# Memory tokens of the last four row tiles: from matrix-engine transposes to strips that the vector engine turns

## The chip, the core and the metric

The kernel runs on one core of a Trainium2 chip. A core has a matrix engine (TensorE, PE in the profile; its weight loads are listed as PEld), a vector engine (VectorE, DVE), a scalar engine (ScalarE, ACT), GpSimd (POOL) and SyncE (SP), which here only issues transfers. Sixteen DMA engines move data between the device's memory and the core's on-chip memory. The metric is device time of one execution in microseconds (us).

## The reference, cut to what matters

Two layers of an encoder over 256 positions of width 2048, each with three groups of heads (a gated convolution, a differential attention, a cross attention into 256 memory tokens). What the change touches is how the memory tokens become keys and values, which depends on `mem` and the weights alone and not on the layer's `x`:

```python
for l in range(DEPTH):                       # DEPTH = 2
    h = rmsnorm(x, norm_g[l]); proj = h @ w_in[l]
    ...
    mn = rmsnorm(mem, mem_norm_g[l])         # mem: 256 x 2048
    mkv = mn @ w_mem_kv[l]                   # 2048 x 1024: 512 columns of keys, 512 of values
    mk = rmsnorm(keys of mkv, per head of 128); mv = values of mkv
    ...                                      # attention of 4 heads into mk, mv
    x = x + y @ w_out[l]
```

All numbers are float32. The kernel multiplies them as pairs of parts, a high one (`hi`, the number rounded to the engine's short format) and a low one (`lo`, the rest), in three products: hi by hi, token lo by weight hi, token hi by weight lo.

## The kernel before

**Three stages.** The first stage makes keys and values of both layers out of the memory tokens (some 97 us, matmuls of line 743, `products`). Then come the two layers, whose matmuls are those of `block` (lines 301 to 303). Every matmul of `block` and of `products` moves 512 columns.

**The first stage** goes over 32 row tiles, named g = 0 to 31: 16 row tiles k of 128 rows of `w_mem_kv` for layer 0, then 16 for layer 1. Row tile g takes 12 matmuls: `products(g, 0, ...)` for the keys' half (two halves of the tokens, times three products) and `products(g, 1, ...)` for the values' half. The order within one g >= 3 is written out by hand: the first two matmuls of the keys' half, then `operands(g + 2)`, then the other four, then `beside(g)`, then six of the values' half, then `run_side()`. For k = 14 and 15, and for the first two row tiles of layer 1, the values' half is moved to a later place.

**`operands(n)`** makes what row tile n multiplies. `token_parts(n)`, for n < 16 alone, brings the tokens into columns: two 128x128 transposes on TensorE (line 721, into tile `pt`), an ACT copy (L252) to `memT`'s hi part and a DVE subtraction (L253) for its lo part. `memT` is kept, so layer 1 needs no token work. `w_parts(n)` scales the weights by the gain: ACT writes `hi` (L715), DVE writes `lo` (L716). ACT and DVE work through their own instructions strictly in this order. There are four buffers each for `raw`, `hi` and `lo`, so SP's load of `raw` for row tile g + 4 (L707, issued in `beside(g)`) waits until DVE has written `lo` of row tile g.

**`beside(g)`** holds what lies next to the products: loads of the tokens, four row tiles at a time (L701, in their natural layout, `xs`), loads of the weights, one small constant at a time from a list (L776), the tokens' squares on ACT (L661, at g = 4, 8, 11 and 13), natural loads of `x` at g = 18, 21, 24, 27 (L764), whose squares (L650) follow three row tiles later, and at g = 4, 9, 14, 19 the start of `x_turned` for one quarter of `x` each. `x`'s squares are not pinned to a place; the planner of the program puts them in ACT's order.

**`x_turned`** brings a quarter of `x` (512 columns) into columns without TensorE: four DMAs (L618) fetch strips (each partition takes pieces of 128 numbers, 512 bytes), two row tiles later one DVE instruction turns them in 32x32 blocks (L622), and in the next two `run_side` calls ACT (L255) and DVE (L256) write hi and lo parts of two column tiles each. Row j of such a tile is row 4p + j of its quarter and not row 128j + p, so the weights that meet it are loaded by `x_row_tiles` in the same order. Tile tags `e` (the strips) and `sh` (the turned tile) have two buffers each.

**The start**: `weights(0)` to `weights(3)` and tokens 0 to 3 are loaded in an order written out by hand; the first row tiles go in halves (`w_parts(g + 1, 0, NB)`, then `w_parts(g + 1, NB, NB)`), while `weights(2)` and `weights(3)` come in one transfer each and tokens 2 and 3 together.

Of the kernel before, what the change touches and what calls it, by code (L numbers as in the profile page):

```python
# [11 lines left out]
F32 = mybir.dt.float32  # L12
# [7 lines left out]
P = 128  # L20
D_MODEL = 2048
SEQ = 256
DEPTH = 2
NT = SEQ // P
KT = D_MODEL // P
# [8 lines left out]
NB = 512  # L34
CK = 2
PARTS = 8
B = 32
NA = P // B
PAIR_EVERY = 9
QT = NB // P  # L40


C_X, C_B, C_C, C_G = 0, 768, 1536, 2304
# [5 lines left out]
def encoder(ctx: ExitStack, tc: tile.TileContext, x, mem, norm_g, w_in, conv_w, conv_b,  # L49
            dq_g, dk_g, lq1, lk1, lq2, lk2, head_g, mem_norm_g, w_mem_kv, mq_g, mk_g, w_out, out):  # L50
    nc = tc.nc
    x, mem, out = x[0], mem[0], out[0]

    def pool(name, bufs, space=None):
        kw = {"space": space} if space is not None else {}
        return ctx.enter_context(tc.tile_pool(name=name, bufs=bufs, **kw))

    const = pool("const", 1)
# [3 lines left out]
    tmp = pool("tmp", 2)  # L62
# [8 lines left out]
    def nm(s):  # L71
        uid[0] += 1
        return f"{s}_{uid[0]}"
# [8 lines left out]
    def distance(t):  # L82
        tc.keep_in_program_order(nc.scalar.activation(dist[:, t], dist[:, t], AF.Abs))
# [13 lines left out]
    def on_all_rows(v):  # L97
        return v.rearrange("l d -> (l d)").unsqueeze(0).to_broadcast([P, DEPTH * HALF])
# [3 lines left out]
    pin = tc.keep_in_program_order  # L102

    def small_loads():

        yield gx.rearrange("p (m j) -> p m j", j=QT), norm_g.rearrange("l (q p j) -> p (l q) j", p=P, j=QT)
        for r0, v in vb_rows:
            n, w = v.shape
            for j in range(P // w):
                yield vb[r0:r0 + n, j * w:(j + 1) * w], v  # L110
        for j, v in enumerate((lq1, lk1, lq2, lk2)):
            yield lam_in[:, j, :], on_all_rows(v)

    constants = small_loads()


# [7 lines left out]
    cva = const.tile([P, 32], F32, name="cva")  # L124

    def g_norm(l, k):
        return gx[:, l * KT + k:l * KT + k + 1]

    def g_mnorm(l, k):
        return cva[:, l * KT + k:l * KT + k + 1]  # L130

    cvb = const.tile([P, 64], F32, name="cvb")
    hgain = const.tile([P, DEPTH], F32, name="hgain")
# [71 lines left out]
    def later(g, n):  # L205
        due[id(g)] = chunk[0] + n
        return g
# [40 lines left out]
    def split_T(dst, k, src, gain, pin=False):  # L248

        hi, lo = dst[:, 0, k, :], dst[:, 1, k, :]  # L250
        if gain is None:
            both = (nc.scalar.copy(hi, src),  # L252
                    nc.vector.tensor_tensor(lo, src, hi.bitcast(F32), ALU.subtract))  # L253
        else:
            both = (nc.scalar.activation(hi, src, AF.Copy, scale=gain),  # L255
                    nc.vector.scalar_tensor_tensor(lo, src, gain, hi.bitcast(F32), ALU.mult, ALU.subtract))  # L256
        if pin:
            for i in both:
                tc.keep_in_program_order(i)
        made.add((id(dst), k))  # L260
# [5 lines left out]
    def x_row_tiles(w, k):  # L266

        q, j = divmod(k, QT)
        return w[q * NB:(q + 1) * NB].rearrange("(p j) c -> p j c", j=QT)[:, j:j + CK]

# [155 lines left out]
    def strips(v):  # L426
        return v.rearrange("p (b c) -> p b c", c=B)
# [180 lines left out]
    def mem_out(h, yn, po, r, a):  # L608
        for i in range(NT):
            nc.vector.scalar_tensor_tensor(yn[:, :, i], strips(po[:, i, :]), r[:, i:i + 1],  # L610
                                           strips(a[:, i, h * P:(h + 1) * P]), ALU.mult, ALU.mult)

    def x_turned(dst, l, q, src):


        st = tmp.tile([P, SEQ // B, B * QT], F32, tag="e", name=nm("xt"))
        for b in range(NA):
            tc.keep_in_program_order(nc.sync.dma_start(  # L618
                st[b * B:(b + 1) * B], src[:, b * B * QT:(b + 1) * B * QT].rearrange("(n p) r -> p n r", p=B)))
        yield 2  # L620
        whole = tmp.tile([P, QT, SEQ], F32, tag="sh", name=nm("xf"))
        tc.keep_in_program_order(nc.vector.transpose(whole.rearrange("p j (n i) -> p j n i", i=B),  # L622
                                                     st.rearrange("p n (c j) -> p j n c", j=QT)))
        yield
        for j in range(QT):
            split_T(dst, q * QT + j, whole[:, j], g_norm(l, q * QT + j), pin=True)
            if j % 2:
                yield
# [13 lines left out]
    def T_tile(what):  # L642
        kept.append(big.tile([P, 2, KT, SEQ], F32R, tag="T", name=nm(what)))
        return kept[-1]
# [9 lines left out]
    memT = T_tile("memT")  # L654
    ssm = const.tile([P, NT, 4], F32, name="ssm")

    def mem_squares(c):

        for t in range(NT):
            sq = tmp.tile([P, NB], F32, tag="nat", name=nm("msq"), bufs=3)  # L660
            pin(nc.scalar.activation(sq, xs[:, t, c * NB:(c + 1) * NB], AF.Square, accum_out=ssm[:, t, c:c + 1]))  # L661
# [35 lines left out]
    mkT, mv, away, raws, parts = [], [], [], {}, {}  # L697
    xT = T_tile("xT")

    def tokens(k, n):  # L700
        pin(nc.sync.dma_start(xs[:, :, k * P:(k + n) * P], mem[:, k * P:(k + n) * P].rearrange("(t p) c -> p t c", p=P)))  # L701

    def weights(g, at=0, n=2 * NB, eng=nc.sync):
        l, k = divmod(g, KT)
        if g not in raws:
            raws[g] = wp.tile([P, CK, NB], F32, tag="raw", name=nm("raw"), bufs=4)
        pin(eng.dma_start(raws[g].rearrange("p h c -> p (h c)")[:, at:at + n],  # L707
                          w_mem_kv[l][k * P:(k + 1) * P, at:at + n]))

    def w_parts(g, at=0, n=2 * NB):  # L710
        if g not in parts:
# [6 lines left out]
    def turned(k):  # L718
        pt = ps_t.tile([P, SEQ], F32, tag="t", name=nm("pt"))
        for t in range(NT):  # L720
            pin(nc.tensor.transpose(pt[:, t * P:(t + 1) * P], xs[:, t, k * P:(k + 1) * P], ident))  # L721
        return pt

    def token_parts(g):
        if g < KT:
            split_T(memT, g, turned(g), None, pin=True)

    def operands(g):
        token_parts(g)
        w_parts(g)  # L730
# [36 lines left out]
    def beside(g):  # L767


        if g + 4 < NG:  # L770
            if g % QT == 0 and g + QT < KT:
                tokens(g + QT, QT)
            weights(g + 4)
        if g >= 3:
            for dst, src in islice(constants, 1):
                pin(nc.sync.dma_start(dst, src))  # L776
        if g in (4, 9, 14, 19):
            q = g // 5
            tasks.append(later(x_turned(xT, 0, q, x[:, q * NB:(q + 1) * NB]), 1))
        if g in (4, 8, 11, 13):  # L780
            mem_squares((4, 8, 11, 13).index(g))
        if g == 6:
            distance(1)
        if g == 13:
            tasks.append(later(mem_stats(), 1))
        if g == 28:
            rest_of_constants()
        if g > KT and (g - KT) % 3 == 2 and g < 30:
            x_natural((g - KT) // 3)
        if g > 20 and (g - KT) % 3 == 2:  # L790
            for t in range(NT):
                x_square((g - KT) // 3 - 1, t)

    for _ in range(DEPTH):
        l = len(mkT)
# [6 lines left out]
    tokens(1, 1)  # L802
    weights(1, 0, NB)
    weights(1, NB, NB)
    tokens(2, 2)
    weights(2)
    weights(3)
    warm(5)
    distance(0)
# [24 lines left out]
    for g in range(3, NG):  # L834
        l, k = divmod(g, KT)
# [19 lines left out]
    for l in range(DEPTH):  # L855
        st = stats_of(ssx, "st")
# [146 lines left out]
        for b in range(4):  # L1003
# [3 lines left out]
            for t in range(NT):  # L1007
                n = 256 if final else NB
                for lo in range(0, NB, n):
                    xc = xs[:, t, b * NB + lo:b * NB + lo + n]  # L1010
                    nc.vector.tensor_tensor(xc, acc[t][:, lo:lo + n], xc, ALU.add)  # L1011
                    if final:
                        eng = nc.scalar if lo else nc.sync
# [36 lines left out]
```

## Time and profile before

| | |
|---|---|
| median of 3 runs | 923.13 us (922.33 to 924.15) |
| the profiled execution's own time | 922.7 us |
| its span, first to last instruction | 920.9 us |
| busy: PE / DVE / ACT | 99% / 73% / 54% of the span |
| bytes moved | 215.06 MB, mean 234 GB/s |
| first stage | from 4.76 us to about 97.4 us |

Times in the trace are us from the span's start. PE's sum of busy time is that of pipelined instructions; the distance from one start to the next says what an instruction costs the engine. A row of the timeline is a start, a length, an engine, a line and an operation, the tile written `<-` the tiles read, and in square brackets the idle time ahead of it with what ended it. A `q` behind the engine's name marks an issue of its queue. The chain of waits gives start, length, engine, tile, line and count.

### The profile page before, as it was taken

To read this page: it belongs to the slowest core of one execution; us is meant where nothing else is said; L and a number is where in the kernel's file an instruction comes from. 1 tells how busy PE (TensorE), PEld (TensorE's weight loads), DVE (VectorE), ACT (ScalarE), POOL (GpSimd) and SP (SyncE) were. 2 spreads that over 40 slices of the span, in tenths; PEclk is the share of its full clock that TensorE was granted. 3 is DMA by queue.
4 is the path that set the end of the run, shared out by engine and by line. 5 is a ranking of instruction groups with operands and counts; after the bars stand their busy time and mean duration, and the time that the engine had idled before them with its cause. 6 is when DMAs were issued, how large, how long until landed. Compare 5 with 4: busy or idle time off the path is not lost.

```text
span 920.9 us, 12319 instructions
## 1 busy us (share of the span) xinstructions
PE 915.9 (99%) x4192; PEld 761.0 (83%) x4192; DVE 671.9 (73%) x1195; ACT 501.9 (54%) x770; POOL 7.0 (1%) x18
## 2 busy tenths in 40 slices
PE   9999999999999999999999999999999999999998
PEld 7888888888888888888888888888888888888886
DVE  5797877857898787467676757878898777468652
ACT  6676645675545554436455544568555554446431
POOL 0001000000000000000000000000000000000000
PEclk9999999999999999999999999999999999999999
DMA  8988877876679997989677767885889897989662
GB/s 280 273 257 298 267 234 231 259 208 197 175 219 243 234 278 235 242 263 257 222 262 241 240 197 218 234 236 182 238 231 223 254 237 209 250 252 262 214 223 68
DMA packets 250226, 215.06 MB, mean 234 GB/s; under 512 B 131166, under 2 KB 176820, under 8 KB 250164
## 3 DMA queue, kind: packets, MB, share of 16 engines
q1 hardware_dynamic: 248004, 210.72, 78.7%
q0 software_dynamic: 672, 2.10, 0.6%
q10 hardware_dynamic: 1488, 1.46, 0.5%
q8 instruction: 33, 0.54, 0.2%
q14 instruction: 29, 0.24, 0.1%
HBM read 193.26 MB, written 20.97 MB: 233 GB/s over the span
## 4 chain that ended last, share of the span: by engine, by line
PE 99%; DVE 0%; DVEq 0%; issue 0%
PE acc L303 28%; PE acc L301 28%; PE acc L302 28%; PE acc L743 10%; PE po L434 2%; PE s L542 1%; PE s L541 1%; PE s L594 1%; PE pt L721 0%; PE warm L122 0%; DVE xs L1011 0%; DVEq L1045 0%; PE pva L811 0%; PE pvb L142 0%
## 5 line engine op out<-in xcount | busy, mean ns | idle before, releaser
L281 DVE TENSOR_TENSOR lo<-raw,hi 128x1024 fp32r<-128x1024 f32 x288 | 351.8, 1222 | 184.1 <-ACT hi L280 179.2
L280 ACT CAST hi<-raw 128x1024 fp32r<-128x1024 f32 x288 | 302.4, 1052 | 325.5 <-PE acc L303 255.0
L302 PE MATMUL acc<-lo,xT 128*128 128x512 f32 x896 | 349.0, 390 | 0.0
L301 PE MATMUL acc<-hi,xT 128*128 128x512 f32 x896 | 348.8, 391 | 0.0
L303 PE MATMUL acc<-hi,xT 128*128 128x512 f32 x896 | 348.7, 389 | 0.0
L303 PEld LDWEIGHTS acc<-hi,xT 128*128 128x128 f32 x896 | 168.2, 188 | 34.7
L301 PEld LDWEIGHTS acc<-hi,xT 128*128 128x128 f32 x896 | 168.2, 188 | 33.9
L302 PEld LDWEIGHTS acc<-lo,xT 128*128 128x128 f32 x896 | 168.3, 188 | 33.7
L301 PE MATMUL acc<-hi,yT 128*128 128x512 f32 x256 | 99.6, 389 | 0.0
L302 PE MATMUL acc<-lo,yT 128*128 128x512 f32 x256 | 99.6, 389 | 0.0
L303 PE MATMUL acc<-hi,yT 128*128 128x512 f32 x256 | 99.6, 389 | 0.0
L743 PE MATMUL acc<-hi,memT 128*128 128x512 f32 (+1 forms) x260 | 73.1, 396 | 0.0
L302 PEld LDWEIGHTS acc<-lo,yT 128*128 128x128 f32 x256 | 48.0, 188 | 10.1
L303 PEld LDWEIGHTS acc<-hi,yT 128*128 128x128 f32 x256 | 48.0, 188 | 10.1
L301 PEld LDWEIGHTS acc<-hi,yT 128*128 128x128 f32 x256 | 48.0, 188 | 9.8
L743 PEld LDWEIGHTS acc<-hi,memT 128*128 128x128 f32 x260 | 47.9, 192 | 9.6 <-ACT hi L715 0.5
L716 DVE SCALAR_TENSOR_TENSOR lo<-raw,cva,hi 128x1024 fp32r<-128x1024 f32 (+2 forms) x37 | 41.7, 1138 | 8.1 <-ACT hi L715 7.8
L715 ACT ACTIVATE hi<-raw,cva 128x1024 fp32r<-128x1024 f32 (+2 forms) x37 | 37.6, 1033 | 9.6 <-DMA raw<-in_w_mem_kv_dram 9.6
L743 PE MATMUL acc<-lo,memT 128*128 128x512 f32 (+1 forms) x130 | 40.1, 390 | 0.0
L743 PEld LDWEIGHTS acc<-lo,memT 128*128 128x128 f32 x130 | 24.5, 190 | 5.2
L552 ACT ACTIVATE e<-e,mx 128x256 f32<-128x256 f32 x48 | 23.8, 499 | 1.4 <-DVE mx L548 1.3
L546 DVE SCALAR_TENSOR_TENSOR e<-dist,s 128x512 f32<-128x512 f32 x24 | 15.7, 681 | 2.3 <-PE s L542 1.9
(151 smaller groups left out, 602.4 us busy)
## 6 DMA issues: line engine op xcount, KB each, us to landing
raw<-in_w_in_dram SPq DMA_DIRECT2D x192, 512.0 KB, 4.0
raw<-in_w_out_dram SPq DMA_DIRECT2D x64, 512.0 KB, 4.3
raw<-in_w_in_dram SPq DMA_DIRECT2D x64, 256.0 KB, 4.5
raw<-in_w_mem_kv_dram SPq DMA_DIRECT2D x30, 512.0 KB, 3.8
d<-sh SPq DMA_DIRECT2D x80, 128.0 KB, 3.8
sh<-d SPq DMA_DIRECT2D x64, 128.0 KB, 4.7
d<-yn SPq DMA_DIRECT2D x40, 64.0 KB, 3.6
yn<-d SPq DMA_DIRECT2D x40, 64.0 KB, 3.4
```

What stands on the lines that cost most here:

```text
L280: nc.scalar.copy(hi, raw)
L281: nc.vector.tensor_tensor(lo_, raw, hi.bitcast(F32), ALU.subtract)
L301: nc.tensor.matmul(acc[t], sh, hi, start=first, stop=False)
L302: nc.tensor.matmul(acc[t], sh, lo, start=False, stop=False)
L303: nc.tensor.matmul(acc[t], sl, hi, start=False, stop=last)
L434: nc.tensor.matmul(po[:, t, :], eT[:, i, t, k, :], v[:, k, h * P:(h + 1) * P], start=k == 0, stop=k == NT - 1)
L541: nc.tensor.matmul(s[c][:, i, :], qi, k_first(yT, c, h), start=True, stop=False)
L546: nc.vector.scalar_tensor_tensor(e[:, c], dist, -slopes[h], s[c], ALU.mult, ALU.add)
L552: nc.scalar.activation(e[:, c, i], e[:, c, i], AF.Exp, bias=mx[:, c, i:i + 1], accum_out=sm[:, c, i:i + 1])
L715: pin(nc.scalar.activation(hi, raw, AF.Copy, scale=gain))
L716: pin(nc.vector.scalar_tensor_tensor(lo, raw, gain, hi.bitcast(F32), ALU.mult, ALU.subtract))
L743: pin(nc.tensor.matmul(accs[l, half][t][:, at:at + n], memT[:, token_part, k, t * P:(t + 1) * P], p, start=k == 0 and at == 0 and token_pa ...
```

## The change

The tokens of row tiles 12 to 15 (`DEALT = 12`) get the treatment that quarters of `x` have. Their strips are loaded at g = 6 (`mem_strips(3)`, four DMAs), DVE turns them at g = 9 (`mem_turned(3)`), and `token_parts` for these four splits the turned tile instead of a `pt` that TensorE made. The weights of these row tiles, in both layers, come in the row order that fits (`x_row_tiles`), and their gain has a tile of its own, `gm_dealt`, loaded by two more constants. Since the constants' list has two more entries ahead, it starts at g = 2 and not at 3. The tokens' natural load of row tiles 12 to 15 is still there (the squares need it), at g = 10 and not at 8. `x`'s first quarter stays at g = 4; the other three move from 9, 14, 19 to 14, 19, 24. At the start, `weights(2)` comes in two halves and tokens 2 and 3 come by one transfer each. `x_turned` is cut into `strips_of` and `strips_turned`, with the same instructions.

```diff
+    gm_dealt = const.tile([P, DEPTH, (KT - DEALT) // QT, QT], F32, name="gm_dealt")
     def g_mnorm(l, k):
-        return cva[:, l * KT + k:l * KT + k + 1]
+        if k < DEALT:
+            return cva[:, l * KT + k:l * KT + k + 1]
+        q, j = divmod(k - DEALT, QT)
+        return gm_dealt[:, l, q, j:j + 1]
...
     def small_loads():
+        for m in range(DEPTH):
+            yield gm_dealt[:, m], mem_norm_g[m, DEALT * P:].rearrange("(q p j) -> p q j", p=P, j=QT)
...
+    def strips_of(src):
         st = tmp.tile([P, SEQ // B, B * QT], F32, tag="e", name=nm("xt"))
         for b in range(NA):
+            pin(nc.sync.dma_start(
                 st[b * B:(b + 1) * B], src[:, b * B * QT:(b + 1) * B * QT].rearrange("(n p) r -> p n r", p=B)))
+        return st
+    def strips_turned(st):
+        whole = tmp.tile([P, QT, SEQ], F32, tag="sh", name=nm("xf"))
+        pin(nc.vector.transpose(whole.rearrange("p j (n i) -> p j n i", i=B),
+                                st.rearrange("p n (c j) -> p j n c", j=QT)))
+        return whole
...
     def weights(g, at=0, n=2 * NB, eng=nc.sync):
-        pin(eng.dma_start(raws[g]...[:, at:at + n], w_mem_kv[l][k * P:(k + 1) * P, at:at + n]))
+        if k < DEALT:
+            rows = w_mem_kv[l][k * P:(k + 1) * P]
+        else:
+            rows = x_row_tiles(w_mem_kv[l], k - k % CK)[:, k % CK]
+        pin(eng.dma_start(raws[g]...[:, at:at + n], rows[:, at:at + n]))
...
     def token_parts(g):
         if g < KT:
-            split_T(memT, g, turned(g), None, pin=True)
+            split_T(memT, g, turned(g) if g < DEALT else dealt[g // QT][:, g % QT], None, pin=True)
...
     def beside(g):
         if g + 4 < NG:
-            if g % QT == 0 and g + QT < KT:
-                tokens(g + QT, QT)
+            if g in (0, 4, 10):
+                tokens({0: 4, 4: 8, 10: 12}[g], QT)
             weights(g + 4)
-        if g >= 3:
+        if g == 6:
+            mem_strips(3)
+        if g == 9:
+            mem_turned(3)
+        if g >= 2:
             for dst, src in islice(constants, 1):
                 pin(nc.sync.dma_start(dst, src))
-        if g in (4, 9, 14, 19):
-            q = g // 5
+        if g in (4, 14, 19, 24):
+            q = (4, 14, 19, 24).index(g)
             tasks.append(later(x_turned(xT, 0, q, x[:, q * NB:(q + 1) * NB]), 1))
...
-    tokens(2, 2)
-    weights(2)
+    tokens(2, 1)
+    weights(2, 0, NB)
+    weights(2, NB, NB)
+    tokens(3, 1)
     weights(3)
```

More of the change, by code (lines that the diff above doesn't have):

```diff
@@ L40 @@
 QT = NB // P
+DEALT = 12
 C_X, C_B, C_C, C_G = 0, 768, 1536, 2304
@@ L611, in mem_out, with x_turned @@
                                            strips(a[:, i, h * P:(h + 1) * P]), ALU.mult, ALU.mult)
-    def x_turned(dst, l, q, src):
+    def strips_of(src):
         st = tmp.tile([P, SEQ // B, B * QT], F32, tag="e", name=nm("xt"))
         for b in range(NA):
-            tc.keep_in_program_order(nc.sync.dma_start(
+            pin(nc.sync.dma_start(
                 st[b * B:(b + 1) * B], src[:, b * B * QT:(b + 1) * B * QT].rearrange("(n p) r -> p n r", p=B)))
+        return st
[4 more added lines that the diff above has]
+        return whole
+    def x_turned(dst, l, q, src):
+        st = strips_of(src)
         yield 2
-        whole = tmp.tile([P, QT, SEQ], F32, tag="sh", name=nm("xf"))
-        tc.keep_in_program_order(nc.vector.transpose(whole.rearrange("p j (n i) -> p j n i", i=B),
-                                                     st.rearrange("p n (c j) -> p j n c", j=QT)))
+        whole = strips_turned(st)
         yield
@@ L706, in weights @@
             raws[g] = wp.tile([P, CK, NB], F32, tag="raw", name=nm("raw"), bufs=4)
-        pin(eng.dma_start(raws[g].rearrange("p h c -> p (h c)")[:, at:at + n],
-                          w_mem_kv[l][k * P:(k + 1) * P, at:at + n]))
+        if k < DEALT:
+            rows = w_mem_kv[l][k * P:(k + 1) * P]
+        else:
+            rows = x_row_tiles(w_mem_kv[l], k - k % CK)[:, k % CK]
+        pin(eng.dma_start(raws[g].rearrange("p h c -> p (h c)")[:, at:at + n], rows[:, at:at + n]))
     def w_parts(g, at=0, n=2 * NB):
@@ L722, in turned, with mem_strips, mem_turned @@
         return pt
+    dealt = {}
+    def mem_strips(q):
+        dealt[q] = strips_of(mem[:, q * NB:(q + 1) * NB])
+    def mem_turned(q):
+        dealt[q] = strips_turned(dealt[q])
     def token_parts(g):
         if g < KT:
-            split_T(memT, g, turned(g), None, pin=True)
+            split_T(memT, g, turned(g) if g < DEALT else dealt[g // QT][:, g % QT], None, pin=True)
     def operands(g):
```

## The prediction

> **What bounds the kernel now.** I read the shares and the ends of the waits first: is there an engine that never waits? Then the chain of waits around the row tiles that change, for the period of one row tile.
>
> The granted clock in 40 slices, and the shares of the chain that ended last:
>
> ```profile
> PEclk9999999999999999999999999999999999999999
> ```
>
> ```profile
> PE 99%; DVE 0%; DVEq 0%; issue 0%
> ```
>
> TensorE's waits, the whole list; then the chain's longest pieces (start, length) and the transposes' own line (shortest, median and longest in ns):
>
> ```profile
> PE warm L122 <- PEq L1036: 0.8, 1, 0.8
> ```
>
> ```profile
> 39.86 2.77 PE acc L743 x12
> 42.85 2.77 PE acc L743 x12
> 45.85 41.76 PE acc L743 x184
> ```
>
> ```profile
> L721 PE MATMUL pt<-ident,xs x32: 270/271/474, 3.2 to 45.6; 128*128 128x128 f32 x32
> ```
>
> The chain is TensorE from one end to the other, and all that TensorE ever waits is 0.8 us before its first instruction, at the full clock. So the kernel lasts as long as TensorE's instructions do, and a change gains only what it takes off TensorE, and loses whatever makes TensorE wait. The last lines give the price. A row tile with two transposes repeats every 42.85 - 39.86 = 2.99 us. From 45.85, where the transposes end, 184 matmuls take 41.76 us, 0.227 each, so 12 of them 2.72. Two transposes thus cost 2.99 - 2.72 = 0.27 us, 0.135 each, although each one is listed as 0.271 long: they run into one another and into the matmul behind.
>
> **The change part by part.** *Eight transposes fewer* (row tiles 12 to 15): 4 x 0.27 = 1.08 us off TensorE. Whether this arrives depends on ACT and DVE, which must deliver row tile 12 by another road (timelines of PE, ACT and DVE: row tile 12's first matmuls; hi 11, the tokens' copy and hi 12; the turn of x's first quarter, lo 11, the tokens' lo, lo 12):
>
> ```profile
> 42.02 0.62 PE L743 MATMUL acc<-hi,memT 128*128 128x512 f32 x2
> ```
>
> ```profile
> 34.77 1.16 ACT L715 ACTIVATE hi<-raw,cva 128x1024 fp32r<-128x1024 f32 x1
> 36.90 0.37 ACT L252 CAST memT<-pt 128x256 fp32r<-128x256 f32 x1 [0.97 <-PE pt L721]
> 37.17 1.16 ACT L715 ACTIVATE hi<-raw,cva 128x1024 fp32r<-128x1024 f32 x1
> ```
>
> ```profile
> 28.28 2.04 DVE L622 STREAM_TRANSPOSE xf<-xt 128x1024 f32<-128x1024 f32 x1 [0.61 <-DMA xt<-in_x_dram]
> ...
> 35.96 1.29 DVE L716 SCALAR_TENSOR_TENSOR lo<-raw,cva,hi 128x1024 fp32r<-128x1024 f32 x1 [0.49 <-ACT hi L715]
> 37.31 0.42 DVE L253 TENSOR_TENSOR memT<-pt,memT 128x256 fp32r<-128x256 f32 x1
> 38.36 1.28 DVE L716 SCALAR_TENSOR_TENSOR lo<-raw,cva,hi 128x1024 fp32r<-128x1024 f32 x1 [0.63 <-ACT hi L715]
> ```
>
> *One turn more on DVE.* The new turn is pinned behind lo of row tile 11 (35.96 to 37.25) and costs 2.04 us, the length of x's. Until 39.29 everything behind it on DVE waits, and ACT's copy of row tile 12 too, behind which stands ACT's hi 12. By the rows, hi ends 37.17 + 1.16 - 36.90 = 1.43 us after that copy starts and lo 38.36 + 1.28 - 36.90 = 2.74 us after: hi 12 at 40.7, lo 12 at 42.0 (38.3 and 39.6 before). TensorE starts row tile 12 at 42.02 now, and 2 x 0.27 earlier then, at 41.48 (two pairs of transposes stand ahead of it). It needs hi 12 there and lo 12 after four matmuls, at 42.39. Slack 0.75 and 0.35 us: hidden, but by little, where before it was over 2. From row tile 13 on the tokens lie ready, ACT no longer waits for TensorE, and the slack returns. The four splits read what DVE wrote instead of TensorE's output, same shape, 0.37 and 0.42 us in these rows; I take no difference, and one would vanish in ACT's idle 0.97.
>
> *The strips' loads.* Four issues, 0.4 to 0.5 us each by the issues shown here, stand on SP between the weights of row tiles 10 and 11, in the place of the natural tokens' one, which goes two row tiles later. SP's timeline (weights of row tile 11, natural tokens), the issues' table (KB each, median us to landing) and two windows (after the clock: share of the DMA engines, GB/s):
>
> ```profile
> 25.84 0.35 SPq L707 DMA_DIRECT2D raw<-in_w_mem_kv_dram  x1
> ...
> 27.50 0.39 SPq L701 DMA_DIRECT2D xs<-in_mem_dram  x1
> ```
>
> ```profile
> xt<-in_x_dram SPq DMA_DIRECT2D x16, 128.0 KB, 7.3
> ...
> xs<-in_mem_dram SPq DMA_DIRECT2D x3, 512.0 KB, 5.7
> ```
>
> ```profile
> 23.00:25.00 2.00, 2.00 (x12) 1.61 (x11) 1.28 (x1) 0.43 (x2) 0.00 (x0) 1.00 1.23 185
> 29.00:31.00 2.00, 2.00 (x12) 1.61 (x11) 2.00 (x3) 1.67 (x3) 0.00 (x0) 1.00 1.01 396
> ```
>
> The strips leave at 25.4 to 27.3 and take 7.3 us (x's strips, the nearest row): landed by 34.6, so the turn at 37.25 doesn't wait, by 2.6 us. Who pays is the weights of row tile 11, queued behind them: issued at about 27.6 and not 25.84, after the bytes that lie ahead of the natural tokens today, which land at 27.50 + 5.7 = 33.2. Bounds: 33.2 if strips move like natural tokens, 33.2 + (7.3 - 5.7) = 34.8 by the difference of the two landings. hi 11 starts at 34.77 now, so even the upper end costs about nothing; I take zero, nearer the upper end. The Trainium skill's "DMA: Bandwidth & Descriptors" (Specifications) puts the least transfer for line rate at 512 bytes, which would make the strips as quick as any other load, the lower end; by it the sum stays and the slow rival below would lose its chance. The two windows say otherwise: while x's strips flow (23 to 25) the queues are fully busy at 185 GB/s, without them (29 to 31) at 396. I go by the windows.
>
> *x's quarters move.* The second and third take the places that the third and fourth had; the slot at g = 9 goes (its transfer, turn and splits), which relieves DMA, ACT and DVE from 32 to 49. New is the slot at g = 24. A window, SP's timeline around that slot, and what ACT, DVE and TensorE do late in the stage:
>
> ```profile
> 79.00:81.00 2.00, 2.00 (x10) 1.65 (x10) 2.00 (x3) 2.00 (x6) 0.08 (x1) 1.00 0.29 115
> ```
>
> ```profile
> 73.03 0.39 SPq L764 DMA_DIRECT2D xs<-in_x_dram  x1
> 77.05 5.12 SPq L707 DMA_DIRECT2D raw<-in_w_mem_kv_dram  x3
> 82.26 0.43 SPq L764 DMA_DIRECT2D xs<-in_x_dram  x1
> ```
>
> ```profile
> 89.83 0.63 ACT L650 ACTIVATE sq<-xs 128x512 f32<-128x512 f32 x1 [5.33 <-DMA xs<-in_x_dram]
> ...
> 91.17 1.14 ACT L715 ACTIVATE hi<-raw,cva 128x1024 fp32r<-128x1024 f32 x1
> ```
>
> ```profile
> 87.84 0.23 DVE L167 COPY cvb<-pvb 128x64 f32<-128x64 f32 x1 [2.02 <-PE pvb L142]
> ...
> 92.34 1.28 DVE L716 SCALAR_TENSOR_TENSOR lo<-raw,cva,hi 128x1024 fp32r<-128x1024 f32 x1 [0.16 <-ACT hi L715]
> ```
>
> ```profile
> 94.22 0.62 PE L743 MATMUL acc<-lo,memT 128*128 128x512 f32 x2
> ```
>
> SP is free from 73.4 to 77.0, so the issues fit. DVE's new work is 2.04 for the turn and 4 x 0.42 for the splits, 3.7 us; lo of the row tiles behind it moves later by that less the idle there (2.02 us before 87.84), and row tile 30, whose products end about 93, has it by then; the last quarter is not read before the first layer begins at 97. The tight place is ACT: it stands 5.33 us for x's last natural load (issued 82.26, landed 89.8), with hi 31 queued behind its squares. lo 31 ends at 93.62 and TensorE reads it at 94.22: slack 0.60. Then TensorE comes 1.08 us sooner. If that load keeps its time, 0.48 us of the gain is lost here; if all loads move along with TensorE (they wait for buffers that row tiles free), nothing is. The strips can make it later by 0 (the queues have room, share 0.29 from 79 to 81) to 1.6 us (the landings' difference). I take zero: room beside it and an earlier chain before it, since ACT and DVE lose a whole quarter's work ahead of 49.
>
> *The start, in parts.* Two issues more on SP, about 0.45 us each, ahead of weights 3. ACT's timeline (hi of weights 2's first half, tokens 2, then hi of weights 2's second and weights 3's first half) and TensorE's start on row tile 2:
>
> ```profile
> 10.34 0.72 ACT L715 ACTIVATE hi<-raw,cva 128x512 fp32r<-128x512 f32 x1 [1.21 <-DMA raw<-in_w_mem_kv_dram]
> 11.12 0.38 ACT L252 CAST memT<-pt 128x256 fp32r<-128x256 f32 x1
> 11.39 1.34 ACT L715 ACTIVATE hi<-raw,cva 128x512 fp32r<-128x512 f32 x2
> ```
>
> ```profile
> 11.85 1.11 PE L743 MATMUL acc<-hi,memT 128*128 128x512 f32 x4
> ```
>
> ACT waits 1.21 us for weights 2, and their first half then ends at 11.06, 0.8 ahead of TensorE's need at 11.85. An earlier first half shortens ACT's wait, not TensorE's: zero, and up to 0.5 in an execution where that load comes later. Weights 3's first half is done at 12.73 and read one row tile (2.99) after 11.85, so 0.9 us later costs nothing. *Two more constants and the natural tokens two row tiles later* stand in gaps of SP while it waits for buffers: zero.
>
> **Sum.** 922.7 - 1.08 = 921.6 us for the profiled execution. The median shown, 923.13, is 0.43 above that execution; from it, 922.05, said as 922.0.
>
> **The rivals.**
> *Part of the gain is eaten by a late operand* (lo 12 or lo 31). For: slacks of 0.35 and 0.60, both smaller than the gain. Against: the queues' room, and 2.6 us between the strips' landing and their turn. Price: 0.5 us at row tile 31 with the load at its old time, up to 0.5 + 1.6 = 2.1 with the strips ahead of it: 922.5 to 924.1.
> *Slower by over 0.2%: DVE stands at the turn for late strips.* It is pinned, so lo of every later row tile waits with it. It begins to cost when the strips land after 37.25 + 0.35 = 37.6, makes the kernel slower than before from 38.7, and passes 0.2% (1.85 us) from 40.5. For: the queues are full just then. Against: x's strips in equally full queues took 7.3 us, which gives 34.6. Time at 41: 925.5.
> *A transpose costs its listed length,* 0.271 us each, and TensorE gets 8 x 0.271 = 2.2 us: 920.9, faster by over 0.2%. For: the row of line 721. Against: the period, 2.99 against 2.72. The Trainium skill's "TensorE: Matmul & The Clock Gate" (Part 4: PE-mode transpose) gives about 275 ns in a kernel's context, which the length here matches; it would give this rival's time.
> *Nothing moves,* because something else sets the period in 36 to 46: 923.1. Against: no wait of TensorE anywhere.
>
> **How the numbers follow.** The full gain 0.56, partly eaten 0.27, slow at the turn 0.06, listed length 0.08, nothing 0.03. A difference of 0.2% (1.85 us) is about what a measurement of this kernel can tell from no change. So faster 0.08, same 0.56 + 0.27 + 0.03 = 0.86, slower 0.06. The range 920.9 to 923.4 holds the first, fourth and last cases and most of the second (a loss below 1.4 us); left out are its end and the turn, below 2 in 10.
>
> **What would show it.** Right: 24 instructions of line 721 on TensorE where there were 32, the periods of row tiles 10 to 13 at 2.72, no wait of TensorE beside the first, the span near 919.8. The turn near 37 without a DMA wait before it. Wrong: TensorE starts row tile 12 after 41.5 or pauses before a `lo` matmul near 42.4 or 93.1; hi 11 on ACT later than 35; ACT's squares of x's last quarter after 89.8; or a different order of the unpinned instructions after 97 with waits of TensorE there.

## The result, and the profile after

The changed kernel takes 924.85 us (median of 17; 923.24 to 927.5) against 923.07 of the kernel before on the same chip: a ratio of 1.0022 (1.0016 to 1.0029). The forecast was 922.0, in a range up to 923.4. A second group of 11 (`a0_after_again`, the same code beside the experiments) gave 924.53 against 922.94: 1.0012 (1.0004 to 1.0021). The kernel got slower by 0.1 to 0.2%, by the medians 1.6 to 1.8 us, where a gain of 1.08 had been expected.

The first profiled execution took 926.69 us, 1.8 above its median; the second group's, of the same kernel, took 924.33, 0.2 below its median. So I read places and order in both, and prices in the second. The page of the first: span and the chain's shares.

```profile
span 924.9 us, 12318 instructions
...
PE 90%; DMA 5%; DVE 2%; ACT 2%; issue 1%; SPq 0%; DVEq 0%; ACTq 0%
```

The chain that ended last was 99% TensorE and is now 90%: ten per cent of it runs through DMA, DVE and ACT. The list of TensorE's waits (sum, times, longest) of the first and, behind it, of the second execution:

```profile
PE acc L771 <- ACT hi L735: 1.7, 2, 1.0
PE warm L125 <- PEq L1070: 0.8, 1, 0.8
PE pva L845 <- DMA va<-in_mem_norm_g_dram: 0.5, 1, 0.5
PE acc L771 <- ACT mv L786: 0.4, 1, 0.4
```

```profile
PE acc L771 <- ACT hi L735: 1.3, 1, 1.3
PE warm L125 <- PEq L1070: 0.8, 1, 0.8
```

Before, the 0.8 at the start was all. The wait common to both is for ACT's `hi`; TensorE's timeline shows it at row tile 12, the first of the turned ones (second execution):

```profile
40.17 1.09 PE L771 MATMUL acc<-hi,memT 128*128 128x512 f32 x4
41.09 0.62 PE L771 MATMUL acc<-lo,memT 128*128 128x512 f32 x2
43.02 1.19 PE L771 MATMUL acc<-hi,memT 128*128 128x512 f32 x4 [1.30 <-ACT hi L735]
...
45.83 0.39 PE L771 MATMUL acc<-lo,memT 128*128 128x512 f32 x1
```

From 41.09 to 45.83 lie 12 matmuls: 4.74 us where 2.72 would do, so 2.0 lost at this one place (1.30 for `hi`, the rest in smaller gaps behind it). The balance of the first stage, by the start of the first layer's first matmul, before and in the two executions after (in the order of the fences: before, first, second):

```profile
97.39 0.39 PE L301 MATMUL acc<-hi,xT 128*128 128x512 f32 x1
```

```profile
101.56 0.39 PE L309 MATMUL acc<-hi,xT 128*128 128x512 f32 x1
```

```profile
99.21 0.39 PE L309 MATMUL acc<-hi,xT 128*128 128x512 f32 x1
```

Second execution: 99.21 - 97.39 = +1.82. That is -1.08 for the transposes, +2.0 at row tile 12, +0.8 in gaps near 95, 0.05 at the start, by pauses over 0.227 per matmul; the sum, 1.7, leaves 0.1. What follows is as long as before (span 922.5 - 99.21 = 823.3; before 920.9 - 97.39 = 823.5). Beside that the first execution lost 1.1 at the start (the list has 0.5 of it, a wait for `va`), 1.0 near 58 and 0.6 more near 96, and 0.3 less at row tile 12.

Why `hi` was late is on ACT and DVE (second execution: hi of row tiles 8 to 12 with the copy ahead of the last; lo 11 and the turn):

```profile
26.59 1.15 ACT L735 ACTIVATE hi<-raw,cva 128x1024 fp32r<-128x1024 f32 x1 [1.25 <-DMA raw<-in_w_mem_kv_dram]
...
30.79 1.15 ACT L735 ACTIVATE hi<-raw,cva 128x1024 fp32r<-128x1024 f32 x1 [2.45 <-DMA raw<-in_w_mem_kv_dram]
...
33.70 1.15 ACT L735 ACTIVATE hi<-raw,cva 128x1024 fp32r<-128x1024 f32 x1 [0.70 <-DMA raw<-in_w_mem_kv_dram]
...
37.07 1.15 ACT L735 ACTIVATE hi<-raw,cva 128x1024 fp32r<-128x1024 f32 x1
41.51 0.41 ACT L260 CAST memT<-xf 128x256 fp32r<-128x256 f32 x1 [3.29 <-DVE xf L631]
41.82 1.14 ACT L735 ACTIVATE hi<-raw,gm_dealt 128x1024 fp32r<-128x1024 f32 x1
```

```profile
38.25 1.28 DVE L736 SCALAR_TENSOR_TENSOR lo<-raw,cva,hi 128x1024 fp32r<-128x1024 f32 x1 [0.53 <-ACT hi L735]
39.46 2.02 DVE L631 STREAM_TRANSPOSE xf<-xt 128x1024 f32<-128x1024 f32 x1
```

The turn has no bracket: it did not wait for its strips. It starts where lo 11 ends, and lo 11 is late because hi 11 is (37.07, before 34.77). hi 11's own row has no bracket either, so the trace names no wait for it. Two things end together there: ACT's delay, gathered at hi 8 to 10, which waited 1.25, 2.45 and 0.70 us for weights (before: hi 9 alone, below), and weights 11 themselves, whose last part lands at 36.99 by the trace's landing times. So the question goes to SP. Before, weights 9 on SP and hi 9 on ACT:

```profile
21.41 0.48 SPq L707 DMA_DIRECT2D raw<-in_w_mem_kv_dram  x1
```

```profile
29.33 1.16 ACT L715 ACTIVATE hi<-raw,cva 128x1024 fp32r<-128x1024 f32 x1 [1.04 <-DMA raw<-in_w_mem_kv_dram]
```

And SP in the second execution after:

```profile
18.94 0.43 SPq L808 DMA_DIRECT2D gx<-in_norm_g_dram  x1
19.41 2.60 SPq L625 DMA_DIRECT2D xt<-in_x_dram  x4
22.11 3.32 SPq L728 DMA_DIRECT2D raw<-in_w_mem_kv_dram  x1
25.53 0.39 SPq L808 DMA_DIRECT2D vb<-in_conv_w_dram  x1
26.57 0.36 SPq L728 DMA_DIRECT2D raw<-in_w_mem_kv_dram  x1
27.05 2.09 SPq L625 DMA_DIRECT2D xt<-in_mem_dram  x4
29.32 0.32 SPq L808 DMA_DIRECT2D vb<-in_conv_b_dram  x1
30.77 0.35 SPq L728 DMA_DIRECT2D raw<-in_w_mem_kv_dram  x1
```

The `raw` rows are the weights of row tiles 9, 10 and 11. Two things are new. `gx` (by the code 1024 pieces of 16 bytes) was issued a row tile earlier before; pushed back by the two `gm_dealt` entries, it now stands just ahead of `x`'s strips, and the issue of weights 9 takes 3.32 us (0.48 before). And weights 10 and 11 leave at 26.57 and 30.77, the moments at which ACT's waits for weights 8 and 9 end (26.59, 30.79). Counted by issues, the eighth transfer ahead of weights 11 is weights 9: weights 9, conv_w, weights 10, four strips, conv_b.

The trace also says what SP waits for there. Each issue names the semaphore (a counter that its landing raises), and from 12 us to the end of the first stage SP's issues use eight of them in turn: an issue first waits until the transfer that last used its semaphore has landed, and that is the eighth ahead. In all 14 traces no issue of that stretch leaves before this landing. Before, the eighth ahead of weights 11 was `x`'s first strip, landed at 25.78 (issue at 25.84); now it is weights 9, landed at 30.70 (issue at 30.77).

### The profile page after: what moved, and what is told of

The parts are those of the page before. It is cut to its first block, busy times and chain, and to the rows that moved or that the text cites. A ratio compares the mean times of both kernels' runs of the same rounds, so it can differ in the third digit from the quotient of the medians.

```text
span 924.9 us, 12318 instructions
## 1 busy us (share of the span) xinstructions
PE 917.2 (99%) x4184; PEld 760.6 (82%) x4184; DVE 674.1 (73%) x1196; ACT 501.0 (54%) x770; POOL 7.0 (1%) x18
## 4 chain that ended last, share of the span: by engine, by line
PE 90%; DMA 5%; DVE 2%; ACT 2%; issue 1%; SPq 0%; DVEq 0%; ACTq 0%
PE acc L311 28%; PE acc L309 28%; PE acc L310 28%; PE po L442 2%; DMA xs<-in_x_dram 2%; PE acc L771 1%; DVE lo L736 1%; ACT hi L735 1%; DMA xt<-in_x_dram 1%; DMA raw<-in_w_mem_kv_dram 1%; DMA xt<-in_mem_dram 1%; DMA xs<-in_mem_dram 1%; PE s L550 1%; PE s L549 1%; PE s L602 1%
## 5 line engine op out<-in xcount | busy, mean ns | idle before, releaser
L736 DVE SCALAR_TENSOR_TENSOR lo<-raw,cva,hi 128x1024 fp32r<-128x1024 f32 (+2 forms) x29 | 31.6, 1099 | 8.6 <-ACT hi L735 8.4
L735 ACT ACTIVATE hi<-raw,cva 128x1024 fp32r<-128x1024 f32 (+2 forms) x29 | 28.3, 1001 | 13.1 <-DMA raw<-in_w_mem_kv_dram 13.0
L631 DVE STREAM_TRANSPOSE xf<-xt 128x1024 f32<-128x1024 f32 x9 | 18.2, 2018 | 0.8 <-DMA xt<-in_x_dram 0.8
```

What stands on the lines that cost most here:

```text
L631: pin(nc.vector.transpose(whole.rearrange("p j (n i) -> p j n i", i=B), st.rearrange("p n (c j) -> p j n c", j=QT)))
L735: pin(nc.scalar.activation(hi, raw, AF.Copy, scale=gain))
L736: pin(nc.vector.scalar_tensor_tensor(lo, raw, gain, hi.bitcast(F32), ALU.mult, ALU.subtract))
```

## The experiments

Two theories at first. *SP theory:* the new entries and strips on SP delay the weights, which moves hi 11, lo 11 and the turn. *Last-quarter theory:* the new slot at g = 24 is the trouble, late in the stage. The second part of the first became a theory of its own: *eight under way*, that is, an issue on SP waits until the eighth transfer ahead of it has landed, so that four strips in the place of one load hold the next weights. Every kernel ran beside the kernel before on the same chip (medians of the latter 922.94 to 923.09). Two executions of e8 and one of e10 took over 2000 us, for which nothing here gives a reason; medians do not depend on them. Each run has one profiled execution, and it need not be typical: it is the fastest of its group in e1, e3 and e10 and the slowest in e4 and e6.

**e1_gx_first: `gx` back to its old gap.**

```diff
     def small_loads():
+        yield gx.rearrange(...), norm_g.rearrange(...)
         for m in range(DEPTH):
             yield gm_dealt[:, m], ...
-        yield gx.rearrange(...), norm_g.rearrange(...)
```

> The changed kernel with one edit: in the list of constants x's gains (gx, 1024 pieces of 16 bytes) stand first again and the two gm_dealt behind it, so gx is issued at g = 2 and no longer at g = 4 between the weights of row tile 8 and x's first strips. Theory A (gx in front of the strips holds up SP and the queues): the issue of weights 9 is short again (0.5 us, not 3.46), hi 9 on ACT starts without the 1.88 us wait, the turn starts 2 us earlier relative to TensorE, the wait before row tile 12 falls from 1.2 us to below 0.3, the one at 57 to 58 goes with it; time 922.2 to 922.8 against 924.85. Rival B (the four strip issues themselves take the place of one natural load on SP, which has eight transfers under way at most): weights 11 still late, wait before row tile 12 still above 1 us, time 924.3 or more.

Measured: 925.88, 1.0033 (1.0021 to 1.0044): not better. SP's and ACT's timelines (weights 9, strips, weights 11; hi 9, hi 11):

```profile
21.78 0.40 SPq L728 DMA_DIRECT2D raw<-in_w_mem_kv_dram  x1
...
26.46 2.23 SPq L625 DMA_DIRECT2D xt<-in_mem_dram  x4
...
30.71 0.35 SPq L728 DMA_DIRECT2D raw<-in_w_mem_kv_dram  x1
```

```profile
30.73 1.15 ACT L735 ACTIVATE hi<-raw,cva 128x1024 fp32r<-128x1024 f32 x1 [2.04 <-DMA raw<-in_w_mem_kv_dram]
...
37.44 1.15 ACT L735 ACTIVATE hi<-raw,cva 128x1024 fp32r<-128x1024 f32 x1 [0.63 <-DMA raw<-in_w_mem_kv_dram]
```

The long issue of weights 9 is gone (0.40). Yet weights 11 leave at 30.71, again when weights 9 have landed (hi 9 at 30.73), hi 11 now waits for them itself, and TensorE loses 1.97 us at row tile 12. So `gx` is not the whole cause, and the second part of the SP theory, the strips, does it without `gx`.

**e2_before_gx_at_4: `gx` late in the kernel before.** The rival that `gx` beside strips is enough by itself.

```diff
# on the kernel before
-        yield gx.rearrange(...), norm_g.rearrange(...)
         (behind the first entry of the vb list:)
+                if r0 == 0:
+                    yield gx.rearrange(...), norm_g.rearrange(...)
```

> The kernel before with one edit: gx is issued at g = 4, behind the convolution's weights in the list, so between weights 8 and x's first strips as in the changed kernel. Theory A: the landings of weights 8 and 9 come 2 to 3 us later than before, hi 9 on ACT starts at about 31.5 instead of 29.3; TensorE does not wait or waits less than 0.5 us, since no turn stands behind lo 11; time 923.0 to 923.6 against 923.07. Rival B: nothing moves, hi 9 within 0.5 us of 29.3.

Measured: 922.65, 0.9996 (0.9987 to 1.0004): no change, and below the time forecast. The issues got as long as in the changed kernel (strips 3.88, weights 9 1.93 on SP, here shown with hi 9 on ACT), but TensorE's list keeps its one entry, the 0.8 at the start:

```profile
23.26 1.93 SPq L708 DMA_DIRECT2D raw<-in_w_mem_kv_dram  x1
```

```profile
30.64 1.16 ACT L716 ACTIVATE hi<-raw,cva 128x1024 fp32r<-128x1024 f32 x1 [2.34 <-DMA raw<-in_w_mem_kv_dram]
```

Weights 9 come 1.3 us later than in the profiled execution of before and nobody feels it: the kernel before has that much room. That `gx` made them late is not shown, though: in e9 below, where `gx` has its old gap, hi 9 starts later still (31.12). What the change takes away is the room, 2 us of turn ahead of row tile 12.

**e3_start_undone: the old start.**

```diff
-    tokens(2, 1)
-    weights(2, 0, NB)
-    weights(2, NB, NB)
-    tokens(3, 1)
+    tokens(2, 2)
+    weights(2)
```

> The changed kernel with the start of the kernel before (tokens 2 and 3 in one load, weights 2 in one). Theory A: the later start in the profile (row tile 3 1.1 us later) is the first load's landing and the clock's phase, which vary from run to run: time within 0.5 us of 924.85. Rival C (the two more issues at the start cost that 1.1 us): 923.7.

Measured: 926.28, 1.0034 (1.0021 to 1.0047), 1.4 us above 924.85 and so outside the forecast's 0.5, though its interval overlaps the changed kernel's first; TensorE still loses 1.96 at row tile 12. The old start brings nothing back, so the start in parts is no cause of the loss.

**e4_last_quarter_at_27: the last quarter later still.**

```diff
-        if g in (4, 14, 19, 24):
+        if g in (4, 14, 19, 27):
```

> The changed kernel with x's last quarter started at g = 27 and not 24, so its strips stand behind x's last natural load and its splits behind hi 31. Theory A (strips and splits ahead of hi 31 make the wait before row tile 31's products): the waits at 95.8 and 97.7, together 1.4 us, go; time 923.3 to 923.8 against 924.85. Rival D (the natural load is late because the whole stage's loads are): they stay, 924.6 or more. A further possibility: the quarter then comes too late for the first layer's column tiles 12 to 15 and a new wait opens at 113.

Measured: 926.53, 1.0047 (1.0034 to 1.0059). The wait at row tile 12 stays, the one near 96 stays too (0.8 for `hi`, 1.5 us lost with the gaps behind it), as rival D said, and a new one appears where the layer begins (TensorE's waits):

```profile
PE acc L771 <- ACT hi L735: 2.1, 2, 1.3
PE acc L309 <- ACT kraw L780: 2.1, 1, 2.1
```

The first layer's first matmul waits for an ACT copy (`kraw`) that stands behind the quarter's last splits and behind two conversions of the first layer's weights, which waited 1.78 and 1.77 us for their loads. So lateness in the stage can cost, but whether 24 does is for e9 to say.

**e6_strips_on_pool: the strips off SP.** GpSimd issues them.

```diff
-    def strips_of(src):
+    def strips_of(src, eng=nc.sync):
...
-            pin(nc.sync.dma_start(
+            pin(eng.dma_start(
...
-        dealt[q] = strips_of(mem[:, q * NB:(q + 1) * NB])
+        dealt[q] = strips_of(mem[:, q * NB:(q + 1) * NB], nc.gpsimd)
```

> The changed kernel with the four strips of the memory tokens issued by GpSimd instead of SP; the same bytes at the same place of the program. Theory B (SP's eight transfers under way: with four more issues, weights 11 leave only when weights 9 have landed): weights 11 leave at about 26 instead of 31, hi 11 starts before 36, the wait at row tile 12 falls to 0.5 us or less and the waits behind it with it; time 923.0 to 924.0. Rival E (the bytes: the strips themselves fill the queues): weights 11 leave earlier but land at 37 as in the last runs, wait unchanged, time as the changed kernel's on this chip within 0.5 us. Rival F (GpSimd issues late or slowly, so the turn waits for the strips): a wait of DVE at the turn.

Measured: 926.97, 1.0038 (1.0026 to 1.005); not the gain forecast, by a fault of my edit. GpSimd waits for nothing there and issued the strips at the start of the kernel, among the first loads:

```profile
1.90 2.48 POOL L625 DMA_DIRECT2D xt<-in_mem_dram  x4
```

The start came 2.4 us later. Against that start, hi 11 (38.42) stood at 36.0, and row tile 12 lost 0.96 instead of 2.0: part of the delay went with the strips, but the run as a whole says little. e10 does it properly.

**e7_strips_first and e8_strips_first_x_early: the memory's strips in `x`'s first slot.** The turn is then due two row tiles earlier, behind lo 9, and the strips stand elsewhere among the weights. e8 moves `x`'s quarters forward as well.

```diff
-        if g == 6:
+        if g == 4:
             mem_strips(3)
-        if g == 9:
+        if g == 7:
             mem_turned(3)
...
-        if g in (4, 14, 19, 24):
+        if g in (9, 14, 19, 24):      # e8: (9, 13, 16, 20)
```

> The changed kernel with the memory tokens' strips at g = 4 and their turn at g = 7, in the place of x's first quarter, and x's quarters at g = 9, 14, 19 and 24. Nothing but one quarter's strips then crosses the queues between 17 and 35, as in the kernel before, and the turn stands where the kernel before had one too. Theory A (the turn too close ahead of its use, behind weights that the strips make late): no wait at row tile 12, the transposes' 1.08 us arrives; what is left are waits of 0.4 to 1.4 us near 95 (x's last quarter at 24); time 922.4 to 923.6. Rival G (reading the tokens from strips costs elsewhere, ACT or DVE too busy in 30 to 50): waits of over 1 us in 36 to 50 remain, time above 924.

> As the run before, with x's quarters at g = 9, 13, 16 and 20, so that none stands near x's last natural load at g = 27. Theory A (both waits gone): no wait of TensorE over 0.3 us behind the start, time 921.7 to 922.3, faster than the kernel before by about 1 us. Rival H (three quarters closer together fill the queues in 45 to 65): a wait of 0.5 us or more in 50 to 70, time 922.5 to 924.

Measured, e7: 922.16, 0.9991 (0.9982 to 0.9999), span 919.7. The forecast's 919.8 appears once the turn is out of the way, though weights 9 still have a long issue behind `gx`, and the waits near 95 that were forecast did not come. The edit moves two things at once, the turn and the strips' place among the weights. SP, the turn on DVE, and all that TensorE waits:

```profile
21.16 3.52 SPq L728 DMA_DIRECT2D raw<-in_w_mem_kv_dram  x1
```

```profile
31.84 2.02 DVE L631 STREAM_TRANSPOSE xf<-xt 128x1024 f32<-128x1024 f32 x1
```

```profile
PE warm L125 <- PEq L1070: 0.8, 1, 0.8
```

Measured, e8: 924.97, 1.0021 (1.001 to 1.0032). Row tile 12 is as in e7, but `x`'s second quarter now meets the values of layer 0: ACT stands for DVE's turn with the copies of `mv` (57.66) queued behind the splits. TensorE's waits and ACT's row:

```profile
PE acc L771 <- ACT mv L786: 2.7, 1, 2.7
```

```profile
56.84 0.91 ACT L263 ACTIVATE xT<-xf,gx 128x256 fp32r<-128x256 f32 x2 [1.53 <-DVE xf L631]
```

So the place of a turn decides, for `x`'s as for the memory's; e7 has the last quarter at 24 and no wait there.

**e9_before_last_at_24: the late slot alone, in the kernel before.**

```diff
# on the kernel before
-        if g in (4, 9, 14, 19):
-            q = g // 5
+        if g in (4, 9, 14, 24):
+            q = (4, 9, 14, 24).index(g)
```

> The kernel before with one edit: x's last quarter starts at g = 24 and not 19. Theory A (the last quarter alone eats the slack of 0.60 us that lo 31 had: its splits stand on ACT between the squares of x's last natural load and hi 31, 0.9 us, and its strips ahead of that load): a wait of 0.3 to 1.4 us near 94, time 923.3 to 924.4 against 922.94. Rival I (the late waits of the changed kernel come only from weights that lost their lead at row tile 12): no wait of TensorE, time within 0.3 us of 922.94.

Measured: 923.38, 1.0005 (0.9996 to 1.0013), and no wait of TensorE near 95. The last-quarter theory falls: the slot by itself costs nothing that can be measured.

The run shows one thing more. Its edit touches nothing ahead of g = 19, so up to there it is a second execution of the kernel before. ACT's hi 9 and hi 11 in it:

```profile
31.12 1.15 ACT L715 ACTIVATE hi<-raw,cva 128x1024 fp32r<-128x1024 f32 x1 [2.03 <-DMA raw<-in_w_mem_kv_dram]
...
36.61 1.16 ACT L715 ACTIVATE hi<-raw,cva 128x1024 fp32r<-128x1024 f32 x1
```

They start 1.8 us later than in the profiled execution of before (29.33 and 34.77), with `gx` in its gap and no strips of the memory tokens, and TensorE does not wait.

**e10_gx_first_strips_pool: both SP causes away, the turn where the change has it.** e1's edit, and GpSimd's issue held back: it first copies a column of `dist` into the strips' tile, so that it waits for ACT's work on `dist` at g = 6.

```diff
# with e1's edit
+        if behind is not None:
+            pin(eng.tensor_copy(st[:, 0, 0:1], behind))
...
-        dealt[q] = strips_of(mem[:, q * NB:(q + 1) * NB])
+        dealt[q] = strips_of(mem[:, q * NB:(q + 1) * NB], nc.gpsimd, dist[:, 1, 0:1])
```

> The changed kernel with gx first in the list and the memory tokens' strips issued by GpSimd at the place where SP issues them now (behind the distances' second half, by a small copy into the strips' tile). Theory B (two holds in a row on SP: gx ahead of x's strips makes weights 9 late, and four strip issues make weights 11 wait for the landing of weights 9): with both gone hi 11 starts about 35 (less than 1 us later than in the kernel before), the wait at row tile 12 falls to 0.5 us or less in all, time 922.6 to 923.6. Rival E (the strips' bytes at that moment are enough): hi 11 still at 36.5 or later with a wait for its weights, wait at row tile 12 still over 1 us, time as the changed kernel's, 924.5.

Measured: 923.97, 1.001 (1.0001 to 1.0019); the profiled execution 921.75, span 920.0. Weights 11 on SP, hi 11 to hi 12 on ACT, the turn on DVE:

```profile
26.64 0.35 SPq L730 DMA_DIRECT2D raw<-in_w_mem_kv_dram  x1
```

```profile
35.12 1.16 ACT L737 ACTIVATE hi<-raw,cva 128x1024 fp32r<-128x1024 f32 x1
39.74 0.41 ACT L260 CAST memT<-xf 128x256 fp32r<-128x256 f32 x1 [3.46 <-DVE xf L633]
40.05 1.15 ACT L737 ACTIVATE hi<-raw,gm_dealt 128x1024 fp32r<-128x1024 f32 x1
```

```profile
37.72 1.99 DVE L633 STREAM_TRANSPOSE xf<-xt 128x1024 f32<-128x1024 f32 x1
```

With the four strip issues gone from SP, weights 11 leave at 26.64 while weights 9 are still under way (hi 9 starts at 29.58 here). Row tile 12 loses 0.4 us instead of 2.0, and the turn, the copy and hi 12's end (37.72, 39.74, 41.20) come near the prediction's 37.25, 39.29 and 40.7. So in this execution the strips' place on SP is what held weights 11. GpSimd's strips also leave later than SP's did (28.59 against 27.05), so how much of hi 11 is due to SP's order and how much to the moment of the bytes is not told apart. The median says less: at 923.97 it lies above the forecast and above the kernel before, its interval is hardly different from that of the changed kernel's second group, and the profiled execution is the fastest of the eleven, 2.2 us below it. What takes the others longer stays open; hi 11 as late as in e9, with a slack of 0.75 us at row tile 12, would do it.

**e11_strips_first_gx_first and e12_e11_start_undone: the better version.** e7's edit and e1's together; e12 is that with the old start (e3's edit).

> The version with the strips at g = 4, the turn at g = 7 and x's quarters at 9, 14, 19, 24, and with gx first in the list besides, so that its small pieces leave in a gap. Theory A: weights 9's issue is short (0.5 us and not 3.5), no wait of TensorE behind the start, time 921.6 to 922.2, the same as without the edit or up to 0.4 us less. Rival (gx does not matter once the turn stands early): 922.16 within 0.2.

> The version with the strips first and gx first, and with the start of the kernel before (weights 2 in one transfer, tokens 2 and 3 in one). Theory J (the start in parts takes 1.1 to 1.5 us of waiting off ACT, of which TensorE feels 0 to 0.4 us in the executions where weights 2 come late): ACT waits 1 us or more before hi of weights 2's first half, time 0.1 to 0.5 us above 921.53, and still below the kernel before by about the transposes' 1.08. Rival K (the start in parts makes the whole difference beyond the transposes or more): 922.5 or above.

Measured: e11 921.53, 0.9985 (0.9976 to 0.9994), span 919.5; e12 921.55, 0.9987 (0.9976 to 0.9997). e11 beats the kernel before by 1.6 us and the change by about 3. Whether `gx` has a share in this is open: e7, without that edit, has 0.9991 (0.9982 to 0.9999), and the intervals overlap. TensorE's waits and the first layer's start in e11:

```profile
PE warm L125 <- PEq L1070: 0.8, 1, 0.8
PE acc L771 <- DVE memT L850: 0.2, 1, 0.2
```

```profile
96.19 0.39 PE L309 MATMUL acc<-hi,xT 128*128 128x512 f32 x1
```

96.19 against 97.39 before: 1.2 us sooner. By the medians the start in parts gives and takes nothing (0.02 us between e11 and e12): the prediction's zero, and less than the 0.1 to 0.5 forecast for e12.

## Why the prediction was wrong, by its own steps

- *Eight transposes at 0.135 each, 1.08 us:* right. TensorE has 24 instead of 32 of them (below, after), and where nothing else stalls (e7) a span of 919.7 against the 919.8 forecast. The rival of the listed length, 2.2 us, fails with it.

```profile
L741 PE MATMUL pt<-ident,xs x24: 270/271/474, 3.7 to 34.7; 128*128 128x128 f32 x24
```

- *"Two more constants and the natural tokens two row tiles later stand in gaps of SP while it waits for buffers: zero":* the reason was incomplete, the zero is not refuted. I costed the issues added, not what they displace. The two entries push `gx` out of its gap to between weights 8 and `x`'s strips; weights 9 then take 3.3 us to issue. But no run shows that this costs anything: e2 has it without a loss, and with `gx` back in its gap (e1) weights 9 land no earlier (30.64, with it 30.70 in the second execution; 31.04 in e9).
- *"Who pays is the weights of row tile 11, ... issued at about 27.6 ... I take zero":* the right payer, the wrong size, and the step that failed. Taken at 0, it came out as a hi 11 2.3 us later than forecast and 2.0 us lost on TensorE; the prediction's own sign, "hi 11 on ACT later than 35", came. I added four issues of 0.45 to the old time of 25.84. SP did not issue when its turn came but when the eighth transfer ahead had landed, and the strips count as four. And I had weights 10, just ahead of the strips, as no payer at all: with the strips behind them they took 6.0 to 7.5 us to land (both executions of the change, e1, e3, e4), without 5.0 to 5.6 (before, e2, e9, e10), for a reason that is not told apart. In the second execution both roads end together: hi 11 starts 3.37 behind a late hi 10 (before 3.33) and 0.08 behind the landing of weights 11. In the table the change is the second profiled execution, and in e11 the turn stands two row tiles earlier:

| | forecast | change | e1 | e10 | e11 |
|---|---|---|---|---|---|
| weights 11 leave SP | 27.6 | 30.77 | 30.71 | 26.64 | 27.34 |
| hi 11 starts | 34.77 | 37.07 | 37.44 | 35.12 | 33.70 |
| turn starts on DVE | 37.25 | 39.46 | 39.83 | 37.72 | 32.11 |
| hi 12 ends | 40.7 | 42.96 | 43.33 | 41.20 | 36.20 |
| TensorE loses at row tile 12 | 0 | 2.0 | 1.97 | 0.4 | 0 |

- *"Slack 0.75 and 0.35 us: hidden, but by little":* the arithmetic was right from hi 11 on (the turn 2.4 us behind hi 11, hi 12's end 3.5 behind the turn, in the forecast and in the run). Fed with a hi 11 that came 2.3 later, it gives 2.3 - 0.75, about 1.5 us of wait at `hi`; 1.30 is listed and 2.0 lost with the gaps behind it. But the slack itself was read from one execution. Without any strips of the memory tokens hi 11 comes 1.34 and 1.84 us later in e2 and e9, which the kernel before could afford with its slack of over 2 us and the changed kernel can't: by the same sum, and with TensorE's own start in those two executions allowed for, the turn would have cost 0.7 and 0.8 us there, an estimate. The strips come on top:

| | before | e2 | e9 | e10 (strips on GpSimd) | change, first | change, second | e1 | e3 | e4 |
|---|---|---|---|---|---|---|---|---|---|
| weights 11 leave SP | 25.84 | 27.59 | 28.14 | 26.64 | 31.81 | 30.77 | 30.71 | 31.18 | 31.63 |
| hi 11 starts | 34.77 | 36.11 | 36.61 | 35.12 | 37.83 | 37.07 | 37.44 | 37.38 | 37.87 |

- *The rivals.* "Part of the gain is eaten by a late operand" named the place, and the way to row tile 31 too, but its price stopped at 2.1 and, for row tile 12, came from no term. "DVE stands at the turn for late strips" did not happen: the strips left later than forecast (27.05), and still the turn never waited for them, because lo 11, which the late weights hold up, came later still (strips landed at 35.75, turn at 39.46). The slower outcome came without that wait.
- *x's last quarter at 24, zero:* right by itself (e9, e7, e11), but not for the room that I read in the trace of before. From 79 to 81 the DMA share was 0.29 there; with the quarter at 24 it is 0.98 to 1.28 in the change, e7, e9 and e11 alike, and only the change loses time. In the change the loads behind row tile 12 have lost their lead: from 44 to 46 the share is 0.06 in the first execution (below) and 0.35 in the second, where it was 0.73.

```profile
44.00:46.00 2.00, 1.89 (x8) 1.22 (x8) 2.00 (x3) 2.00 (x4) 0.00 (x0) 1.00 0.06 23
```

  `x`'s last natural load then comes late (its squares start on ACT at 93.59 and 91.24, before at 89.83), and with 0.90 us of the quarter's splits now ahead of it hi 31 starts at 95.73 and 93.37 (before 91.17). This costs 1.4 us near 96 in the first execution and 0.8 near 95 in the second. That these later losses follow from the first is argued, not shown: the five executions with the loss at row tile 12 lose 1.4, 0.8, 0.5 (e1), 0 (e3) and 1.5 (e4) near 95, and 1.0, 0, 0, 1.3 and 1.0 near 58; e7, e9, e10 and e11 lose at most 0.3 in these places.
- *The start, zero:* right (e3, e12).

## What to carry to other kernels

A step that costs nothing by its own length can still spend the room of another: before calling an added issue free, write out the queue's order with it and see which transfer is pushed behind which. Ask of a new pinned instruction not whether its own input is in time but how late the instruction ahead of it may come; here 0.75 us of slack stood behind a chain of three loads. Read such a slack from more than one execution: the instruction ahead started 1.84 us apart in two executions whose code is the same up to there. And when slack is that small, look for an earlier place for the step before anything else: two row tiles earlier turned a loss of 1.6 to 1.8 us into a gain of 0.8, and of 1.6 in the version with `gx` back in its gap besides.

## What was not expected of the hardware and the runs

- In the first stage of this program SP has eight transfers under way and no more. The traces show where the eight comes from: eight semaphores that its issues use in turn, each issue waiting for the landing that its semaphore told of last. Weights 11 leave 0.06 to 0.07 us behind the landing of weights 9, eight transfers earlier, in the changed kernel (both executions) and in e1; with the strips taken off the queue (e10) the eighth ahead is `x`'s first strip, and they leave 2.9 us before weights 9 have landed. Whether the queue itself would take more than eight, no run tests.
- An issue behind many small pieces is long: the issue of weights 9 behind `gx` took 1.36 to 4.01 us (e2, e3, e4, e6, e7, e8, both executions of the change) and 0.40 to 1.17 without (before, e1, e9, e10, e11, e12). The four strips' issue varied from 1.91 to 3.88 us with no such rule: e10 has 3.72 without `gx` near it.
- A load's landing is told in sixteen parts, and the last can lag. Fifteen parts of weights 8 had landed at 24.66 in before and at 23.97 in the second execution of the change, the sixteenth at 24.94 and 26.51; in e9, the same code as before up to there, at 24.91 and 27.30. Since the next issue waits for the last part, such a lag passes on; nothing here says what makes it.
- The beginning of the kernel differed by 1.1 us between the two profiled executions of the same code; one profile is not enough to price a difference of that size.
